# Opening of a diffusion trunk: the first four k-slices of four row tiles' query, key and value products between the adaLN products, and 256 rows of x loaded later

## The chip, the cores and the metric

The kernel runs on one core of one Trainium2 chip. The metric is device microseconds of one execution. Before the change three runs took 2756.55, 2757.89 and 2761.49 us; the median is 2757.89 us.

## The reference

A trunk of two layers over 1024 latent rows (x, 1024 channels) and 256 context rows. Layer 0 mixes by neighbourhood attention, layer 1 by sliding-window attention; each ends with a gated ConvFFN. Only the beginning of layer 0 matters here:

```python
mod = silu_c @ w_mod[i] + b_mod[i]
mod_c = silu_cc @ w_mod[i] + b_mod[i]
sh1, sc1, gt1, sh2, sc2, gt2 = jnp.split(mod[:, None, :], 6, axis=-1)
h = modulate(rmsnorm(x, g_attn[i]), sh1, sc1)
hc = modulate(rmsnorm(ctx, g_attn[i]), sh1c, sc1c)
q, k, v = attn_inputs(h, w_in, gq, gk, n_kv)
q_c, k_c, v_c = attn_inputs(hc, w_in, gq, gk, n_kv, with_q=not last)
```

So every row of h needs the shift and scale (sh1, sc1), which come out of a product with the 1024 x 2048 left part of w_mod, and every product of queries, keys and values sums over all 1024 channels of h.

## The kernel before

**Tiling.** Rows stand in ten tiles of 128: tiles 0 to 7 are x, 8 and 9 the context. Channels stand in eight slices of 128 (kt 0 to 7, `KT`). Float32 products are made of three passes: each operand is split into a rounded part and a rest (`whi`, `wlo` of the weights, `h0hi`, `h0lo` of h for x, `h0chi`, `h0clo` for the context), and hi*hi, lo*hi and hi*lo are summed in one PSUM bank. `plan_qkv_mm` plans a row tile's product for one pair of heads: eight steps kt of three matmuls of 384 columns, into a bank `mm`. Ten tiles make a head pair (`hp`), eight pairs make the layer; `ORDER` is 8, 9, 0, ..., 7.

**Opening** (the block that opens the pool `x0`, L883 on). The list `so` holds its steps. `plan_x` loads row tiles, sums their squares (ScalarE, `junk<-xt`), scales the rows (`times`), transposes them to channels by rows and evicts them to `x`; it does so for the context (8, 9) and for tiles 0 to 3 together. `plan_mods(half)` multiplies SiLU(c) with eight 512 KB pieces `wm` of w_mod; half 0 gives shift and scale for kt 0 to 3, half 1 for kt 4 to 7; the sum goes through ScalarE (`modsb`), a transpose (`modt`) and VectorE (`modc`). `plan_apply` turns `x` into `h0hi` and `h0lo` for one kt: an affine step, a cast and a subtraction. Four weight pieces of the first head pair (`slab`, two kt each) are loaded and split there too, the first two ahead of the second half of w_mod, the others behind it.

**After the opening** the list `sc` runs: the products of all row tiles, the attention of each head pair, and, ahead of them, `plan_norm0`, which brings tiles 4 to 7 (loaded behind everything else) to `h0hi` and `n1lo`: four sums of squares, four row scalings, eight groups of four transposes into banks `pt`, eight evictions with shift and scale (`t`, the last two into `S`), eight casts, eight subtractions. Its subtractions all wait for the last transpose, since `n1lo` takes the place of the rows themselves.

**What sets the order.** `Sched.op` records a step with an engine (or several to choose from), an assumed duration, what it reads and writes, and a key; `Sched.run` takes the steps as their inputs come free, smallest key first, and writes out one fixed order for each engine. At run time each engine goes through its order and waits where an input is late. DMAs stand in one queue, SP's, in the order of their keys.

Of the kernel before, what the change touches and what calls it, by code (L numbers as in the profile page):

```python
# [17 lines left out]
P = 128  # L18
D = 1024
# [204 lines left out]
def trunk_kernel(ctx, tc, xtok, xseq, cc, crow, wmod, wmodt, bmod, gnorm, na_wqkv, na_gqk, na_bias, na_wo,  # L224
# [29 lines left out]
    dma.dma_start(cpad[:, :, 0:2], cc)  # L254
# [16 lines left out]
    act.activation(cpad[:, :, 0:2], cpad[:, :, 0:2], AF.Silu)  # L271
# [181 lines left out]
    def plan_qkv_mm(sc, key, psa, h, tt, slabs, s, J, c0=0, hkey=None):  # L453

        hh, hl = h[tt // 4]
        sl = slice((tt % 4) * P, (tt % 4) * P + P)
        for kt in range(KT):
            def mm(e, kt=kt):
                if kt == 0:
                    J["acc"] = psa("mm", F32)  # L460
                wh, wl = [a[:, kt % 2, c0:384] for a in slabs.get(4 * s + kt // 2)]
                for i, (a, w) in enumerate(((hh, wh), (hl, wh), (hh, wl))):
                    pe.matmul(J["acc"][:, c0:384], a[:, kt, sl], w, start=(kt == 0 and i == 0),
                              stop=(kt == KT - 1 and i == 2))
# [3 lines left out]
                  acq=[("mm", J["id"] + ("acc",), 1)] if kt == 0 else (), rel=[("w", i)] if kt % 2 else ())  # L468
# [207 lines left out]
    def plan_norm0(sc, psa, wk, junk, xt, hl, key):  # L676

        B = {}
        K = lambda *a: ("n1",) + a

        def sq(e, q):
            if q == 0:
                for s in "vyt":
                    B[s] = tiny.tile([P, 4], F32, tag="n1" + s, name="n1" + s, bufs=1)
            act.activation(junk, xt[q], AF.Square, scale=1.0 / 32.0, accum_out=B["v"][:, q:q + 1])
        for q in range(4):
            sc.op("act", t_act(D) + 0.19, lambda e, q=q: sq(e, q), reads=[("x1", q)] + ([K("ms", q - 1)] if q else []),
                  writes=[K("ms", q)], key=key, rel=["sums1"] if q == 3 else [])
# [11 lines left out]
        def times(e, q):  # L700
            if e == "act":
                act.activation(xt[q], xt[q], AF.Copy, scale=B["y"][:, q:q + 1])
            else:
                dve.tensor_scalar(out=xt[q], in0=xt[q], scalar1=B["y"][:, q:q + 1], scalar2=None, op0=ALU.mult)
        for q in range(4):
            sc.op(("dve", "act"), (0.8, t_act(D)), lambda e, q=q: times(e, q), reads=[K("y")], writes=[("x1", q)], key=key)
        for k in range(KT):
            hi, ring = hl[0][:, k, :], "pt5" if k < 6 else "S"
            shift, scale = modc[:, 0, 0, 0, k:k + 1], modc[:, 0, 0, 1, k:k + 1]

            def tr(e, k=k):
                B["p", k] = psa("pt", F32)
                for q in range(4):
                    pe.transpose(B["p", k][:, q * P:(q + 1) * P], xt[q][:, k * P:(k + 1) * P], idf)
            sc.op("pe", 0.44, tr, reads=[("x1", q) for q in range(4)], writes=[K("tr", k)], key=key, acq=[("pt", K("tr", k), 1)])

            def t(e, k=k, ring=ring, shift=shift, scale=scale):
                if ring == "S":
                    B["t", k] = SP["pool"].tile([P, SP["n"]], F32, tag="S", name="S", bufs=SBUFS)[:, :512]
                else:  # L720
                    B["t", k] = wk.tile([P, 512], F32, tag="pt5", name="t", bufs=PTB["pt5"])
                if e == "act":
                    act.activation(B["t", k], B["p", k], AF.Identity, bias=shift, scale=scale)
                else:
                    dve.tensor_scalar(out=B["t", k], in0=B["p", k], scalar1=scale, scalar2=shift, op0=ALU.mult, op1=ALU.add)
            sc.op(("act", "dve"), (t_actp(512), t_dve(512)), t, reads=[K("tr", k)], writes=[K("t", k)], key=key, rel=[K("tr", k)],
                  acq=[(ring, K("t", k), 1)])

            def hif(e, k=k, hi=hi):
                if e == "act":  # L730
                    act.activation(hi, B["t", k], AF.Copy)
                else:
                    dve.tensor_copy(hi, B["t", k])
            sc.op(("act", "dve"), (t_act(512), 0.45), hif, reads=[K("t", k)], writes=[K("hi", k)], key=key)
        for k in range(KT):
            def lof(e, k=k):
                if k % 2 == 0:
                    hl[1].tiles[k // 2] = lo_part("n1lo")
                dve.tensor_tensor(out=hl[1][:, k, :], in0=B["t", k], in1=hl[0][:, k, :].bitcast(F32), op=ALU.subtract)
            sc.op("dve", t_dve(512), lof, reads=[K("hi", k)] + [K("tr", j) for j in range(KT)] + ([("h0", 1, k - 1)] if k % 2 else []),  # L740
                  writes=[("h0", 1, k)], key=key, rel=[K("t", k)])
# [141 lines left out]
    with tc.tile_pool(name="x0", bufs=1, reuse_waits="tile") as xp, \  # L883
            tc.tile_pool(name="ps0", bufs=1, space=PS, reuse_waits="tile") as ps:
        CUT = {2: (8, 9), 0: (0, 1, 2, 3)}
        xc = {0: hpool.tile([P, KT, 512], F32, tag="hhi", name="x0", bufs=2),
              2: xp.tile([P, KT, TC], F32, name="x2")}
        xt = {i: xp.tile([P, D], F32, tag="xt", name=f"xt{i}", bufs=6) for c in (2, 0) for i in CUT[c]}
        tiny.tile([P, 32], F32, name="pad", bufs=1)
# [14 lines left out]
        for n, i in enumerate((8, 9)):  # L904
            load(1.34, -100 + n, [("xt", i)], lambda i=i: dma.dma_start(xt[i], xtok[i]))
        load(0.3, -98, [("bg",)], lambda: (dma.dma_start(bmod_t, bmod), dma.dma_start(gn, gnorm)))
        for i in range(4):
            load(1.34, -95 + i, [("xt", i)], lambda i=i: dma.dma_start(xt[i], xtok[i]))
# [16 lines left out]
        def tr_bank():  # L925
            return ps.tile([P, 512], F32, tag="tr", name="tr", bufs=4)

        def plan_x(c):
            tl, n, b = CUT[c], CH[c][1], 10 * (c == 0)
# [3 lines left out]
            def sq(e, q, i):  # L933
# [3 lines left out]
                act.activation(junk, xt[i], AF.Square, scale=1.0 / 32.0, accum_out=MS[c, "v"][:, q:q + 1])  # L937
# [1719 lines left out]
```

## Time and profile before

| | |
|---|---|
| profiled execution, device time | 2756.76 us |
| its span | 2754.6 us |
| median of three runs | 2757.89 us |
| TensorE (PE) busy | 2695.8 us, 98% |
| VectorE (DVE) busy | 2247.3 us, 82% |
| ScalarE (ACT) busy | 1685.4 us, 61% |
| GpSimd (POOL) busy | 339.9 us, 12% |
| mean of the 16 DMA engines | 141 GB/s |

The busy shares are means over stages that differ. In the first of the page's 40 slices of 69 us PE is busy for seven tenths and the DMA engines move 263 GB/s; in nearly all others PE is at nine tenths or more. A timeline gives the start, the length and the name of an instruction or of a run of equal ones, and in brackets how long the engine was idle before it and what ended that. Instructions on one engine overlap a little: their pace is the distance of two starts, not the length.

### The profile page before, as it was taken

Reading aid. Unit: us, or ns where it says so; the run is one execution under the profiler, and the core shown is the slowest. Engines: PE = TensorE matmul, PEld = TensorE weight load, DVE = VectorE, ACT = ScalarE, POOL = GpSimd, SP = SyncE. Lnnn points to the kernel's source line nnn. Section 1 sums busy time; section 2 is a strip of 40 time slices with the busy share of each in tenths; the row PEclk is TensorE's granted clock in tenths of the full one; section 3 lists DMA queues with packets and bytes.
Section 4 is the critical chain, followed back from the end, with each engine's and each line's share of the span. In section 5 each row is a group of like instructions: output and inputs, shape, how many; then the busy total and the mean of one; then the engine's idle time right before and its main releaser. Section 6 shows DMA issues by size and latency. Waiting matters only on the chain.

```text
span 2754.6 us, 42728 instructions
## 1 busy us (share of the span) xinstructions
PE 2695.8 (98%) x15300; PEld 2277.4 (83%) x15300; DVE 2247.3 (82%) x4938; ACT 1685.4 (61%) x3000; POOL 339.9 (12%) x520
## 2 busy tenths in 40 slices
PE   7999999998999999999999999999999999999999
PEld 5999999987799988887888877777778788888887
DVE  5988888887788688787886889898877988888757
ACT  6777777776456555555564556666754666656433
POOL 1211111112000000000001007455410000000000
PEclk9999999999999999999999999999999999999999
DMA  7343343325656543334375662143253233334655
GB/s 263 98 127 120 114 136 117 111 91 175 211 173 185 183 142 106 128 118 134 123 252 190 191 197 68 43 129 102 77 154 110 88 115 101 112 108 147 230 174 187
DMA packets 149180, 387.89 MB, mean 141 GB/s; under 512 B 21476, under 2 KB 34276, under 8 KB 148584
## 3 DMA queue, kind: packets, MB, share of 16 engines
q1 hardware_dynamic: 148968, 385.17, 43.2%
q8 instruction: 120, 1.97, 0.3%
q14 instruction: 92, 0.75, 0.1%
HBM read 318.12 MB, written 66.99 MB: 140 GB/s over the span
## 4 chain that ended last, share of the span: by engine, by line
PE 66%; DVE 5%; DMA 2%; issue 1%; POOL 1%; ACT 1%; SPq 0%; DVEq 0%; ACTq 0%; POOLq 0%
PE ua L51 17%; PE uc L51 13%; PE dn L51 13%; PE mm L51 5%; PE oacc L51 4%; PE pt L51 4%; PE ud L51 4%; PE dnc L51 2%; PE s L51 2%; DVE S L51 1%; DVE wlo L51 1%; DVE xn L51 1%; PE ug L51 0%; POOL qa L51 0%; DMA c_dram<-cx 0%
## 5 line engine op out<-in xcount | busy, mean ns | idle before, releaser
L51 ACT ACTIVATE whi<-wraw 128x512 fp32r<-128x512 f32 (+1 forms) x264 | 212.3, 804 | 149.6 <-PE uc L51 57.5
L51 DVE TENSOR_TENSOR wlo<-wraw,whi 128x512 fp32r<-128x512 f32 (+1 forms) x264 | 240.8, 912 | 46.6 <-ACT whi L51 46.1
L51 ACT ACTIVATE S<-S,m 128x640 f32<-128x640 f32 (+3 forms) x288 | 220.8, 768 | 63.4 <-DVE m L51 44.9
L51 PE MATMUL dn<-ghi,whi 128*128 128x512 f32 x616 | 240.2, 390 | 0.1
L51 PE MATMUL dn<-glo,whi 128*128 128x512 f32 x616 | 239.9, 389 | 0.2 <-DVE glo L51 0.2
L51 PE MATMUL dn<-ghi,wlo 128*128 128x512 f32 x616 | 239.8, 389 | 0.0
L51 ACT ACTIVATE whi<-s 128x1024 fp32r<-128x1024 f32 (+1 forms) x118 | 111.0, 941 | 181.5 <-PE uc L51 99.7
L51 POOL TENSOR_TENSOR qy<-qv,mhalf 128x4 f32<-128x4 f32 (+1 forms) x114 | 135.3, 1188 | 597.7 <-DVE qv L51 572.6
L51 PE MATMUL pt<-idr,S 128*128 128x128 f32 x1288 | 194.3, 277 | 12.1 <-DVE S L51 6.1
L51 PEld LDWEIGHTS pt<-idr,S 128*128 128x128 f32 x1288 | 151.2, 141 | 46.9 <-issue 11.7
L51 ACT ACTIVATE ghi<-graw 128x512 fp32r<-128x512 f32 x154 | 95.8, 629 | 150.9 <-PE dn L51 91.2
L51 PE MATMUL mm<-whi,h0hi 128*128 128x384 f32 x512 | 180.1, 352 | 0.0
L51 ACT ACTIVATE pt<-pt 128x512 f32<-128x512 f32 (+2 forms) x259 | 133.4, 535 | 64.6 <-PE pt L51 62.7
L51 PE MATMUL mm<-wlo,h0hi 128*128 128x384 f32 x512 | 172.1, 336 | 0.0
L51 DVE TENSOR_TENSOR glo<-graw,ghi 128x512 fp32r<-128x512 f32 x154 | 105.0, 690 | 80.9 <-ACT ghi L51 50.9
L51 DVE TENSOR_TENSOR wlo<-s,whi 128x1024 fp32r<-128x1024 f32 (+1 forms) x118 | 127.0, 1078 | 21.2 <-ACT whi L51 20.8
L51 PEld LDWEIGHTS dn<-ghi,whi 128*128 128x128 f32 x616 | 115.6, 188 | 24.9 <-ACT ghi L51 0.5
L51 PEld LDWEIGHTS dn<-glo,whi 128*128 128x128 f32 x616 | 115.7, 188 | 24.4 <-DVE glo L51 0.5
L51 PE MATMUL ua<-t12hi,whi 128*128 128x512 f32 x344 | 134.8, 392 | 0.8 <-ACT c L51 0.8
L51 PEld LDWEIGHTS dn<-ghi,wlo 128*128 128x128 f32 x616 | 115.6, 188 | 24.1
L51 PE MATMUL ua<-t12lo,whi 128*128 128x512 f32 x344 | 134.0, 390 | 0.0
L51 PE MATMUL ua<-t12hi,wlo 128*128 128x512 f32 x344 | 133.9, 389 | 0.0
(372 smaller groups left out, 8291.3 us busy)
## 6 DMA issues: line engine op xcount, KB each, us to landing
wraw<-in_w_up_dram SPq DMA_DIRECT2D x133, 512.0 KB, 3.8
wmt<-in_wmodt_dram SPq DMA_DIRECT2D x96, 512.0 KB, 4.1
wraw<-in_w_down_dram SPq DMA_DIRECT2D x44, 512.0 KB, 3.8
graw<-g_dram SPq DMA_DIRECT2D x44, 512.0 KB, 4.4
wraw<-in_w_down_dram SPq DMA_DIRECT2D x88, 256.0 KB, 3.0
graw<-g_dram SPq DMA_DIRECT2D x66, 256.0 KB, 2.7
wm<-in_wmod_dram SPq DMA_DIRECT2D x32, 512.0 KB, 8.7
slab<-in_na_wqkv_dram SPq DMA_DIRECT2D x32, 384.0 KB, 3.1
```

What stands on the lines that cost most here:

```text
L51: r = f(*a, **k)
```

## The change

The context and tiles 0 and 1 are prepared in the opening as before; tiles 2 and 3 no longer are. Their rows are loaded behind w_mod, and a second use of `plan_norm0` brings them to h after the opening (`c == "b"`, groups of two row tiles, 256 columns per kt). The step list of the opening gets half of `plan_qkv_mm` (kt 0 to 3) for tiles 8, 9, 0 and 1 (`EARLY`); they hold two banks `mm` and two banks `s` until the second list adds kt 4 to 7. For that the PSUM pool of the attention is opened before the opening. Slabs 2 and 3 get keys inside the second half of w_mod, `cr` and `cpad` (the two rows of c) are loaded behind the context rows. The squares of tiles 4 to 7 get key 2.5 in place of -100. The subtractions may go to POOL as well.

```diff
-        CUT = {2: (8, 9), 0: (0, 1, 2, 3)}
+    EARLY, EA = {8: 'mm', 9: 'mm', 0: 's', 1: 's'}, {}
+        CUT = {2: (8, 9), 0: (0, 1)}
...
-        dma.dma_start(cr, crow)
-        act.activation(cr, cr, AF.Silu)
+        load(0.2, -99, [("cr",), ("cp",)], lambda: (dma.dma_start(cr, crow), dma.dma_start(cpad[:, :, 0:2], cc)))
+        so.op("act", 1.05, lambda e: act.activation(cr, cr, AF.Silu), reads=[("cr",)], writes=[("cr",)], key=-10)
...
-        for i in range(4):
-            load(1.34, -95 + i, [("xt", i)], lambda i=i: dma.dma_start(xt[i], xtok[i]))
+        for i in range(2):
+            load(1.34, -78 + i, [("xt", i)], lambda i=i: dma.dma_start(xt[i], xtok[i]))
...
-            load(1.0, (-80, -79, -60, -59)[i], [("raw", i)], lambda i=i: slabs.load(i), acq=[("raw", ("raw", i), 2)])
+            load(1.0, (-80, -79, -72.5, -68.5)[i], [("raw", i)], lambda i=i: slabs.load(i), acq=[("raw", ("raw", i), 2)])
-        for i in range(4, 8):
+        for i in range(2, 8):
             load(1.34, -55 + i, [("xt", i)], lambda i=i: dma.dma_start(xt[i], xtok[i]))
...
+        plan_sums0(so, junk, xt, (2, 3), "b", 39)
+        for tt, tag in EARLY.items():
+            J = EA[tt] = dict(id=("q0", 0, tt))
+            plan_qkv_mm(so, 100 + 10 * (tt < 8) + tt % 4, psa, h, tt, slabs, 0, J, 0, ("h0", tt // 4), tag, 0, KT // 2)
         so.run()
...
+        early = hp == 0 and tt in EARLY
+        J = EA[tt] if early else dict(id=I)
+        if early:
+            sc.hold(EARLY[tt], I + ("acc",), 1)
+        plan_qkv_mm(sc, key, psa, h, tt, slabs, hp, J, 0, hkey, k0=KT // 2 if early else 0)
...
-            sc.op("dve", t_dve(512), lof, reads=[K("hi", k)] + [K("tr", j) for j in range(KT)] + ([("h0", 1, k - 1)] if k % 2 else []),
-                  writes=[("h0", 1, k)], key=key, rel=[K("t", k)])
+            sc.op(("dve", "pool"), (t_dve(512), 1.4 * t_pool(512)), lof, reads=[K("hi", u)] + ([K("tr", j) for j in range(KT)] if c == 1 else []) +
+                  ([("h0", 1, u - 1)] if c == 1 and u % 2 else []), writes=[("h0", c, u * m + a) for a in range(m)], key=key,
+                  rel=[K("t", u)])
...
-    plan_norm0(sc, psa, wk, sums0, [xt[i] for i in range(4, 8)], h[1], -100)
+    plan_norm0(sc, psa, wk, xt, h, (2, 3), "b", -150)
+    plan_sums0(sc, sums0, xt, (4, 5, 6, 7), 1, 2.5, ["sums1"])
+    plan_norm0(sc, psa, wk, xt, h, (4, 5, 6, 7), 1, 2.5, [("n0", "b", "tr", u) for u in range(KT // 2)])
```

The planner moves many instructions. Buffer names follow the source: `pt`, `s`, `mm` and `pv` are PSUM banks, `cpad` is SiLU(c), `modsb` the sum of a half of w_mod's products.

PE around the last piece of w_mod, before:

```order
L51 MATMUL mod_327<-wm_368,cpad 32x256 x4
L51 MATMUL mod_327<-wm_377,cpad 32x256 x4
L51 MATMUL modt<-idr,modsb_401 128x128 x2
L51 MATMUL mm<-whi,h0chi 128x384
L51 MATMUL mm<-whi,h0clo 128x384
L51 MATMUL mm<-wlo,h0chi 128x384
```

and with the change (wm_388 is the last piece, h0hi_119 belongs to tiles 0 to 3):

```order
L51 MATMUL s<-whi,h0hi_119 128x384
L51 MATMUL s<-whi,h0lo_121 128x384
L51 MATMUL s<-wlo,h0hi_119 128x384
L51 MATMUL pt<-wm_388,cpad 32x256 x4
L51 MATMUL s<-whi,h0hi_119 128x384
L51 MATMUL s<-whi,h0lo_121 128x384
L51 MATMUL s<-wlo,h0hi_119 128x384
L51 MATMUL s<-whi,h0hi_119 128x384
L51 MATMUL s<-whi,h0lo_120 128x384
L51 MATMUL s<-wlo,h0hi_119 128x384
L51 MATMUL pv<-idr,modsb_427 128x128 x2
```

Before, the first product of h stands behind the last product of w_mod; now all 24 of the context and nine of tiles 0 and 1 stand ahead of it, and six more between it and its transpose.

ACT behind the sum of the second half (`modsb`), before:

```order
L51 ACTIVATE whi<-slab 128x768 x2
L51 ACTIVATE x_111<-x_111,modc 128x256 x2
L51 ACTIVATE h0chi<-x_111 128x256 x2
L51 ACTIVATE x_111<-x_111,modc 128x256
L51 ACTIVATE x_110<-x_110,modc 128x512
```

and with the change (x_108 holds tiles 2 and 3 here, x_109 the context):

```order
L51 ACTIVATE modsb_427<-pt 128x256
L51 ACTIVATE junk,nbv<-x_108 128x1024 x2
L51 ACTIVATE h0chi<-x_109 128x256
L51 ACTIVATE x_109<-x_109,modc 128x256
L51 ACTIVATE h0chi<-x_109 128x256 x2
L51 ACTIVATE x_108<-x_108,modc 128x256 x2
L51 ACTIVATE h0hi_119<-x_108 128x256
L51 ACTIVATE x_108<-x_108,nby 128x1024
```

The two splits of slabs have gone ahead of `modsb`; two sums of squares, of tiles 2 and 3, stand there now, and a row scaling further on.

PE where tile 3 is done and tiles 4 to 7 come up, before (x_119 to x_122 are tiles 4 to 7):

```order
L51 MATMUL mm<-wlo,h0hi_123 128x384
L51 MATMUL pt<-idr,x_119 128x128
L51 MATMUL pt<-idr,x_120 128x128
L51 MATMUL pt<-idr,x_121 128x128
L51 MATMUL pt<-idr,x_122 128x128
```

and with the change (x_115 to x_118 are tiles 4 to 7, the last product is tile 3's last):

```order
L51 MATMUL mm<-wlo,h0hi_119 128x384
L51 MATMUL s<-kkc,q 128x256
L51 MATMUL s<-klc,q 128x256
L51 MATMUL s<-kkc,q 128x256
L51 MATMUL s<-klc,q 128x256
L51 MATMUL pt<-idr,x_115 128x128
L51 MATMUL pt<-idr,x_116 128x128
L51 MATMUL pt<-idr,x_117 128x128
L51 MATMUL pt<-idr,x_118 128x128
```

Before, the transposes stand between the products of tiles 2 and 3; now all 32 stand behind them, with the first scores of the context, and the products of tile 4 follow. On ACT a table load stands between the evictions of these transposes, and three of the eight subtractions stand on POOL. Behind the first head pair (from about the 660th row of PE's order and the 350th of DVE's) both orders are the same to the end.

## Rows read from the trace of the kernel before

**Rows 1.** Busy time by stretch: us; busy (instructions) of PE, PEld, DVE, ACT, POOL; clock, DMA, GB/s
```profile
15.00:20.00 5.00, 3.28 (x38) 1.09 (x30) 2.10 (x7) 2.57 (x3) 1.01 (x1) 1.00 1.05 395
...
25.00:30.00 5.00, 2.25 (x30) 1.39 (x26) 4.30 (x14) 5.00 (x11) 0.00 (x0) 1.00 1.05 388
...
35.00:39.70 4.70, 3.53 (x26) 0.89 (x27) 0.00 (x0) 0.72 (x2) 0.00 (x0) 0.50 1.04 404
39.70:45.00 5.30, 5.30 (x26) 5.30 (x25) 4.54 (x15) 5.30 (x12) 0.00 (x0) 0.78 0.74 294
...
400.00:500.00 100.00, 100.00 (x697) 91.91 (x696) 87.40 (x309) 74.78 (x176) 14.50 (x14) 1.00 0.41 131
```

**Rows 2.** Timeline of SP's DMA issues, opening: start us, us, queue, line, what
```profile
0.74 0.37 SPq L51 DMA_DIRECT2D cr<-in_crow_dram  x1
...
1.86 1.11 SPq L51 DMA_DIRECT2D xt<-in_xtok_dram  x2
```

**Rows 3.** Timeline of PE around the last pieces of w_mod
```profile
36.48 1.08 PE L51 MATMUL mod<-wm,cpad 128*32 128x256 f32 x8 [0.27 <-DMA wm<-in_wmod_dram]
37.83 1.08 PE L51 MATMUL mod<-wm,cpad 128*32 128x256 f32 x8 [0.27 <-DMA wm<-in_wmod_dram]
...
39.75 0.67 PE L51 MATMUL mm<-whi,h0chi 128*128 128x384 f32 x1
...
41.82 0.42 PE L51 MATMUL mm<-whi,h0chi 128*128 128x384 f32 x1
```

**Rows 4.** Timeline of PE from the transposes of tiles 4 to 7 to tile 4
```profile
59.09 1.04 PE L51 MATMUL pt<-idr,x 128*128 128x128 f32 x8
...
70.53 0.33 PE L51 MATMUL mm<-wlo,h0hi 128*128 128x384 f32 x1
70.70 0.33 PE L51 MATMUL mm<-whi,h0hi 128*128 128x384 f32 x1
...
73.82 0.28 PE L51 MATMUL s<-kkc,q 128*128 128x256 f32 x1
...
74.29 0.34 PE L51 MATMUL mm<-whi,h0hi 128*128 128x384 f32 x1
```

**Rows 5.** Timeline of ACT, 27 to 77 us
```profile
27.36 1.08 ACT L51 ACTIVATE x<-x,modc 128x256 f32<-128x256 f32 x2
28.35 0.71 ACT L51 ACTIVATE h0chi<-x 128x256 fp32r<-128x256 f32 x2
...
47.42 1.04 ACT L51 ACTIVATE sums<-x 128x1024 f32<-128x1024 f32 x1
...
48.46 0.47 ACT L51 ACTIVATE qraw<-mm 128x384 f32<-128x384 f32 x1
...
56.51 1.14 ACT L51 ACTIVATE x<-x,n1y 128x1024 f32<-128x1024 f32 x1
...
64.72 0.78 ACT L51 ACTIVATE S<-pt,modc 128x512 f32<-128x512 f32 x1
65.39 0.48 ACT L51 ACTIVATE qraw<-mm 128x384 f32<-128x384 f32 x1
...
75.52 1.28 ACT L51 ACT_TABLE_LOAD   x1
76.82 0.51 ACT L51 ACTIVATE S<-S,m 128x256 f32<-128x256 f32 x1
```

**Rows 6.** Timeline of DVE: the subtractions of tiles 4 to 7, and two equal casts
```profile
66.92 3.09 DVE L51 TENSOR_TENSOR n1lo<-t,h0hi 128x512 fp32r<-128x512 f32 x5
...
95.15 1.43 DVE L51 CAST kll<-kll 64x256 fp32r<-64x256 f32 x1
...
97.25 0.29 DVE L51 CAST kll<-kll 64x256 fp32r<-64x256 f32 x1
```

**Rows 7.** Timeline of POOL, 94 to 99 us
```profile
94.62 1.81 POOL L51 TENSOR_TENSOR wlo<-slab,whi 128x768 fp32r<-128x768 f32 x1 [1.37 <-ACT whi L51]
```

**Rows 8.** Timeline of PE, 96 to 98 us
```profile
97.08 0.33 PE L51 MATMUL pt<-idr,S 128*128 128x128 f32 x1 [1.48 <-DVE kll L51]
```

More of the change, by code (lines that the diff above doesn't have):

```diff
@@ L451, in plan, with plan_qkv_mm @@
                   writes=[("wl", i)], key=key - 2, rel=[("raw", i)])
[L453 to L455 removed]
+    def plan_qkv_mm(sc, key, psa, h, tt, slabs, s, J, c0=0, hkey=None, bank="mm", k0=0, k1=KT):
         sl = slice((tt % 4) * P, (tt % 4) * P + P)
[L457 removed]
+        for kt in range(k0, k1):
             def mm(e, kt=kt):
                 if kt == 0:
[L460 removed]
+                    J["acc"] = psa(bank, F32)
+                hh, hl = h[tt // 4]
                 wh, wl = [a[:, kt % 2, c0:384] for a in slabs.get(4 * s + kt // 2)]
@@ L707, in plan_norm0 @@
[L707 to L719, printed above, removed]
-                else:
-                    B["t", k] = wk.tile([P, 512], F32, tag="pt5", name="t", bufs=PTB["pt5"])
+                dve.tensor_scalar(out=xt[i], in0=xt[i], scalar1=B["y"][:, q:q + 1], scalar2=None, op0=ALU.mult)
@@ L729, in hif @@
-            def hif(e, k=k, hi=hi):
-                if e == "act":
-                    act.activation(hi, B["t", k], AF.Copy)
-                else:
[L733 to L739, printed above, removed]
-            sc.op("dve", t_dve(512), lof, reads=[K("hi", k)] + [K("tr", j) for j in range(KT)] + ([("h0", 1, k - 1)] if k % 2 else []),
-                  writes=[("h0", 1, k)], key=key, rel=[K("t", k)])
+                    dve.tensor_copy(hi, tv(u))
@@ new lines, in plan_norm0, with lof @@
+            sc.op(("act", "dve"), (t_act(512), 0.45), hif, reads=[K("t", u, a) for a in range(m)] + list(after)
+                  + ([K("hi", 0)] if u else []), writes=[K("hi", u)], key=key)
+        for u in range(KT // m):
+            def lof(e, u=u):
+                hl = h[tl[0] // 4]
+                if c == 1:
+                    if u % 2 == 0:
+                        hl[1].tiles[u // 2] = lo_part("n1lo")
+                    lo = hl[1].tiles[u // 2][:, u % 2:u % 2 + 1, :]
+                else:
+                    lo = hl[1].tiles[u][:, :, c0:c0 + n]
+                ENG[e].tensor_tensor(out=lo, in0=tv(u), in1=cols(hl[0], u).bitcast(F32), op=ALU.subtract)
+            sc.op(("dve", "pool"), (t_dve(512), 1.4 * t_pool(512)), lof, reads=[K("hi", u)] + ([K("tr", j) for j in range(KT)] if c == 1 else []) +
+                  ([("h0", 1, u - 1)] if c == 1 and u % 2 else []), writes=[("h0", c, u * m + a) for a in range(m)], key=key,
+                  rel=[K("t", u)])
@@ L892, in trunk_kernel @@
         h = [hi_lo("h0", 0), None, hi_lo("h0", 2)]
-        junk = xp.tile([P, D], F32, name="junk")
+        junk = [xp.tile([P, D], F32, name="junk") for _ in range(2)]
         cr = xp.tile([P, D], F32, name="cr")[0:2]
-        dma.dma_start(cr, crow)
-        act.activation(cr, cr, AF.Silu)
-        so = Sched(dict(tr=4, raw=3, wm=12))
-        so.op("dma", 2.5, lambda e: None, key=-1000)
+        so = Sched(dict(PSB, raw=3, wm=12))
+        so.op("dma", 1.5, lambda e: None, key=-1000)
         def load(dur, key, w, f, **kw):
```

162 lines of the change are left out of this document (103 added, 59 removed).

## The prediction

> **What bounds the kernel now.** I read the page first (PE 98% busy, the others well below), then the busy time by stretch, then the timelines of SP, PE, ACT, DVE and POOL up to 100 us, then the order of both programs. From the second head pair on PE is the bound: it is busy for 100.00 of the 100 us from 400 to 500 [rows 1]. The opening is bound by loads: the pieces of w_mod land 1.35 us apart, PE takes each one as it lands, and from 35 to 39.7 us all that PE does is wait for the next [rows 1, 3]. The first product of h starts at 39.75, and for two more us the products run slowly. So PE time before 39.75 is free, and what the change puts there is PE work out of a stage in which PE is the bound. The question is whether PE can use what it saves. For that I look at the next place where it needs something new: tile 4, whose first product starts at 70.70 [rows 4].
>
> **The loads.** The first row tile is issued at 0.74 instead of 1.86 us, since the two small loads of c go behind it [rows 2]: 1.1 us. Ahead of the last piece of w_mod stood six row tiles, sixteen pieces of 512 KB and two slabs of 384 KB; now there are four, sixteen and four, 256 KB less, at 1.35 us for 512 KB [rows 3] another 0.7 us. The small loads have to pass all the same, 0.2 us. The last piece should start its product at 37.83 - 1.6 = 36.2 us, within 0.9 to either side. SP's order has one new wait: slab 3 needs slab 0's buffer, so it waits for a subtraction on DVE, with the last piece of w_mod queued behind it. By my count that subtraction ends about 2 us before SP gets there, so I cost it at nothing; if that cover went, each us of it would delay everything below by one.
>
> **PE's own side.** A product pass takes 0.17 us at full clock [rows 4]. 48 passes of the first four kt of four tiles move ahead of 39.75; nine of them stand behind the last transpose of the modulation, so 39 are done, 6.7 us. Against that, 16 transposes of tiles 2 and 3 come behind, at about 0.13 us each by the eight in 1.04 us [rows 4]: 2.1 us. There are two new waits, because h for kt 4 to 7 of the context is now needed at once, where before eight us of products covered it: I put them at 1.6 us. With the earlier loads PE alone would reach the end of tile 3 four to five us ahead.
>
> **ACT's side, which I take to decide.** Tile 4 needs the whole of the second `plan_norm0`, and ACT carries most of it. In the new order ACT, once the modulation is summed, first takes the squares of tiles 2 and 3, which land 1.35 us behind the last piece, so from about 37.6 us. From there to its last eviction for tiles 4 to 7 its order holds six sums of squares at 1.04 us (6.2), three affine steps of 256 columns at 0.5 (1.5), seven casts of 256 at 0.31 (2.2), three row scalings at 1.1 (3.3), six evictions of 512 columns at 0.67 (4.0), two casts of 512 at 0.5 (1.0), six evictions of 256, which no row shows: between the cast's 0.31 and the affine step's 0.5, I take 0.45, nearest to the latter (2.7). Add eighteen small steps on queries and keys of the other tiles, at the 384-column eviction's 0.47 less the 0.1 by which neighbours overlap (6.7), the table load at 1.28 and one exponential at 0.5 (1.8) [rows 5]. Sum 29.4 us. With 1.5 us of waits, for the load of tile 3's rows and for transposes, ACT is through at 68.5 us. The first subtraction and tile 4's first product follow at about 69.1.
>
> Before, that product started at 70.70, with the same products and transposes done but not the eight score passes of the context, which stand ahead of it now: four of them take 0.47 us [rows 4], so 0.94. The gain at that point is 1.6 + 0.94 = 2.5 us, not the four to five that PE alone would have.
>
> **Two smaller terms.** The eight subtractions ran on DVE, five in 3.09 us [rows 6]; three of them go to POOL, which needed 1.81 us for 768 columns [rows 7], so 1.2 us each for 512. While POOL worked on that piece, DVE's cast took 1.43 us where an equal one took 0.29 [rows 6, 7]; DVE has two such casts between POOL's subtractions now. Tile 4's products want a new kt each 0.52 us, so PE loses between 0.4 and 1.7 us here; I take 1.0, midway. On the other hand the POOL subtraction at 94.62 is the one that held DVE up and led to PE's stall of 1.48 us at 97.08 [rows 7, 8]; in the new order POOL has no slab there. DVE has it instead, at 0.95 us, so what is won is between nothing and 1.5 us; I take 0.8.
>
> **The sum.** 2.5 - 1.0 + 0.8 = 2.3 us. Bounds with the 0.9 us of the loads: 2.5 - 1.7 - 0.9 = -0.1 and 2.5 - 0.4 + 1.5 + 0.9 = 4.5 us. Behind the first head pair every engine's order is what it was and PE is the bound, so the shift passes to the end. Against the profiled execution that is 2756.76 - 2.3 = 2754.5 us. The median of the runs stands 1.1 us above that execution, so I forecast **2755.6 us**, with the case's own bounds at 2753.4 and 2758.0.
>
> ACT gets a second table load at its start, because the squares now run ahead of the SiLU; the load-bound stretch behind covers its 1.28 us. The load in the middle of the evictions is the one that costs. In the row the exponential starts 0.02 us after the table load ends [rows 5], so I cost it at 1.28. The Trainium skill says more (ScalarE: Activation LUTs, "What ACT_TABLE_LOAD costs"): a switch of sets is the load of about 1283 ns and a drain of about 1380 ns. By that the gain would be some 0.9 us instead of 2.3. The trace agrees on the load and shows no drain of that size behind it.
>
> **The rivals.**
> (a) *PE decides, not ACT.* If ACT's small steps cost less than I count, or DVE takes evictions over in its idle time, PE reaches tile 4 by its own work: from 38.3 us, 105 passes (18.1), 56 transposes at 0.13 (7.3), the scores (0.9), waits of 1.6 make 66.2, a gain of 70.7 + 0.9 - 66.2 = 5.4, with the stall of rows 8 up to 6.9 us: 2752.5 to 2751.0. For it: PE has the work in hand. Against it: ACT is in order and its sum leaves no room for four us.
> (b) *The early products hold up the weights.* PE takes its order strictly, and nine passes stand between the last two pieces of w_mod. From 25 to 30 us PE was busy for 2.25 of 5 us; after that its granted clock fell, to 0.50 from 35 to 39.7 us, which is 1.2 GHz [rows 1]. At that clock a piece takes 1.08 us [rows 3], nine passes at 0.32 us 2.9, more than the 1.35 between two pieces: the last one would start 1.6 us late, which takes the loads' gain away. 2.3 - 1.6 = 0.7: 2757.2 us. For it: PE is idle for some us in the new order too, while it waits for the first context h. Against it: from 24 us on it has more to do than before.
> (c) *Slower.* Between tiles 3 and 4 PE now runs dry: the transposes come as fast as ACT empties two banks, where before they stood among products. If PE's clock falls there, tile 4 begins at 1.2 GHz. Before, the low clock lasted from the dense work's start at 37.83 to 41.82 [rows 3], 4.0 us, at half the pace: a loss of 2.0 us. With the loads no earlier (tile 4 at 70.7), it is 0.94 - 2.0 - 1.0 = -2.1 us: 2760.0 us. It decides if tile 4 begins after 69.6 us at the low clock. For it: eight us at less than half load. Against it: from 15 to 20 us PE was busy for 3.28 of 5 us and the clock stayed at 1.00 [rows 1]. The Trainium skill (TensorE: Matmul & The Clock Gate, Part 1) has the throttled state as the default, released by activity, which speaks for this rival; by that rule alone the price is the same 2.0 us.
>
> **How the numbers follow.** Forecast 0.60, (a) 0.12, (b) 0.14, (c) 0.14. A measurement of this kernel tells about 0.2%, 5.5 us, from no change: below 2752.4 counts as faster, above 2763.4 as slower. The forecast, (b) and most of (c) lie between. Of (a) most is faster by more, 0.10, and a tail of the forecast adds 0.02: faster 0.12. Slower by more needs (c) with a late slab 3 on top: 0.03. Same 0.85. The three runs before spread over 5 us, so medians of three move by 1 to 2; the range is the forecast's bounds widened by 1.7 us on either side and stretched to the near end of (a): 2751.0 to 2759.7.
>
> **What would show it.** Right: the last piece's product at 36 us, squares of `nbv` on ACT at 37 to 40, the clock at full before 38, tile 3's last product at about 60, then PE mostly idle with transposes among ACT's evictions, the first `n1lo` product near 69, and no stall at 97. Wrong: `n1lo` products at 66 (a), the last piece at 37.8 behind slow passes (b), 384-column passes 0.32 us apart behind 69 us (c), or orders that agree while PE's waits past 100 us differ by more than 1 us.

## The result, and the profile after the change

Over 22 runs the changed kernel took 2762.65 us in the median, the kernel before 2758.03 over as many beside it: a ratio of 1.0017, with an interval of 1.0011 to 1.0024. It is slower by some 4.6 us, less than the 0.2% named in the prediction; 2762.65 lies above the prediction's upper bound of 2759.7. The profiled execution of the changed kernel took 2761.46 us, its span is 2759.7 us; PE 2706.4 us busy, DVE 2248.8, ACT 1686.0, POOL 346.4.

Busy time by stretch, changed kernel, columns as in [rows 1]:

```profile
20.00:25.00 5.00, 1.87 (x11) 0.99 (x11) 4.25 (x13) 4.61 (x9) 0.60 (x1) 0.52 1.04 394
25.00:30.00 5.00, 5.00 (x40) 2.88 (x32) 1.76 (x6) 1.99 (x2) 0.10 (x1) 0.80 1.04 389
...
35.00:39.70 4.70, 4.70 (x36) 3.34 (x35) 0.96 (x1) 1.83 (x3) 0.00 (x0) 1.00 1.03 410
...
65.00:70.00 5.00, 3.28 (x17) 2.31 (x17) 3.19 (x9) 4.85 (x10) 0.00 (x0) 0.79 0.00 0
70.00:75.00 5.00, 3.55 (x18) 2.57 (x17) 4.71 (x6) 4.48 (x11) 3.42 (x3) 0.86 0.00 0
```

Before, PE was busy without a gap from 40 to 80 us. Now it is saturated from 25 to 40 us instead, and runs dry from 65 to 75, while ACT is at 4.85 of 5 us. The clock falls twice: from 20 to 30 us, and around 70.

Timeline of PE, changed kernel:

```profile
23.13 0.69 PE L51 MATMUL mm<-whi,h0chi 128*128 128x384 f32 x1 [3.59 <-ACT h0chi L51]
...
35.58 0.64 PE L51 MATMUL pt<-wm,cpad 128*32 128x256 f32 x8
36.15 0.45 PE L51 MATMUL s<-whi,h0hi 128*128 128x384 f32 x1
...
37.94 0.64 PE L51 MATMUL pt<-wm,cpad 128*32 128x256 f32 x8
...
61.52 0.34 PE L51 MATMUL mm<-wlo,h0hi 128*128 128x384 f32 x1
...
67.97 3.14 PE L51 MATMUL pt<-idr,x 128*128 128x128 f32 x12 [1.12 <-ACT t L51]
...
71.65 0.42 PE L51 MATMUL mm<-whi,h0hi 128*128 128x384 f32 x1
72.42 0.44 PE L51 MATMUL mm<-whi,n1lo 128*128 128x384 f32 x1 [0.35 <-DVE n1lo L51]
...
74.79 0.44 PE L51 MATMUL mm<-whi,n1lo 128*128 128x384 f32 x1 [1.04 <-DVE n1lo L51]
...
76.48 0.44 PE L51 MATMUL mm<-whi,n1lo 128*128 128x384 f32 x1 [0.37 <-DVE n1lo L51]
```

Tile 3 is done at 61.52, nine us earlier than before [rows 4]. But the last piece of w_mod still starts its product at 37.94 (37.83 before [rows 3]), nine early passes behind the piece ahead of it, and tile 4 starts at 71.65, 0.95 us later than before, with the eight scores of the context done. Its 24 passes then wait three times for `n1lo`.

ACT, whose chain leads to tile 4:

```profile
38.92 1.05 ACT L51 ACTIVATE junk<-x 128x1024 f32<-128x1024 f32 x1
...
65.36 1.28 ACT L51 ACT_TABLE_LOAD   x1
66.65 0.51 ACT L51 ACTIVATE S<-S,m 128x256 f32<-128x256 f32 x1
...
71.15 0.78 ACT L51 ACTIVATE S<-pt,modc 128x512 f32<-128x512 f32 x1
```

The subtractions of tiles 4 to 7, on DVE and on POOL:

```profile
71.02 1.35 DVE L51 TENSOR_TENSOR n1lo<-t,h0hi 128x512 fp32r<-128x512 f32 x1
...
72.96 4.66 DVE L51 TENSOR_TENSOR n1lo<-t,h0hi 128x512 fp32r<-128x512 f32 x4
```
```profile
70.55 1.27 POOL L51 TENSOR_TENSOR n1lo<-t,h0hi 128x512 fp32r<-128x512 f32 x1 [5.76 <-PE pt L51]
72.85 3.02 POOL L51 TENSOR_TENSOR n1lo<-S,h0hi 128x512 fp32r<-128x512 f32 x2 [1.03 <-DVE h0hi L51]
```

On DVE one took 0.62 us before [rows 6]. Beside POOL's, the one at 71.02 takes 1.27 us to the next start and the first two of the four at 72.96 take 1.69 and 1.70; the last two, behind the end of POOL's work at 75.87, take 0.60 again.

**A measure for what follows.** Orders differ from kernel to kernel, so equal times don't mean equal work. *PE's lag* at a time t is t less the work that PE has begun by then, each instruction counted with the usual distance of two starts for its shape (0.173 us for 384 columns, 0.109 us for a transpose); extra passes of an experiment are not counted as work. The table's columns give the lag less that of the kernel before at the same time: negative is ahead. It wavers by some tenths with the mix of instructions; behind 250 us orders agree for most kernels and it is the difference in time.

| kernel | lag at 40 | 60 | 80 | 530 us | median, us | ratio to before (interval) |
|---|---|---|---|---|---|---|
| changed | -4.7 | -4.3 | +3.3 | +4.1 | 2762.65 | 1.0017 (1.0011 to 1.0024) |
| x13 changed, again | -4.7 | -4.3 | +3.6 | +4.1 | 2760.87 | 1.0011 (1.0002 to 1.0019) |
| x1 subtractions on DVE | -3.8 | -3.4 | +3.1 | +3.8 | 2759.56 | 1.0005 (0.9996 to 1.0014) |
| x2 no early products | -1.4 | +1.5 | +3.1 | +3.5 | 2760.04 | 1.0006 (0.9998 to 1.0015) |
| x4 dry stretch filled | -3.7 | -3.3 | +4.0 | +4.2 | 2758.13 | 1.0004 (0.9995 to 1.0013) |
| x5 squares twice | -3.5 | -2.0 | +5.7 | +5.5 | 2763.95 | 1.0024 (1.0015 to 1.0034) |
| x7 squares on DVE | -4.2 | -3.6 | +7.1 | +4.7 | 2763.92 | 1.0024 (1.0015 to 1.0033) |
| x8 norm first | -3.3 | -2.5 | +2.4 | +4.2 | 2761.27 | 1.0011 (1.0002 to 1.0020) |
| x9 early exponential | -3.5 | -2.9 | +2.7 | +4.2 | 2759.95 | 1.0008 (0.9999 to 1.0017) |
| x10 opening filled | -5.3 | -4.7 | +2.7 | +4.1 | 2759.89 | 1.0009 (1.0000 to 1.0018) |
| x11 three mends | -5.3 | -4.9 | +0.2 | +1.1 | 2759.10 | 1.0003 (0.9994 to 1.0012) |
| x14 mends, context only | -2.0 | -0.7 | -0.1 | +2.0 | 2757.61 | 1.0000 (0.9991 to 1.0009) |
| x18 mends, norm first | -3.9 | -3.4 | +1.0 | +2.7 | 2756.77 | 0.9999 (0.9990 to 1.0008) |

So the place of most of the loss is plain: the changed kernel is 4.3 us ahead at 60 us and 3.3 behind at 80. Behind that the lag still grows in most kernels, by up to 2.1 us (x14) to 530 us.

### The profile page after: what moved, and what is told of

The parts are those of the page before. It is cut to its first block, busy times and chain, and to the rows that moved or that the text cites. A ratio compares the mean times of both kernels' runs of the same rounds, so it can differ in the third digit from the quotient of the medians.

```text
span 2759.7 us, 42763 instructions
## 1 busy us (share of the span) xinstructions
PE 2706.4 (98%) x15300; PEld 2282.1 (83%) x15300; DVE 2248.8 (81%) x4948; ACT 1686.0 (61%) x3008; POOL 346.4 (13%) x524
## 4 chain that ended last, share of the span: by engine, by line
PE 78%; DVE 7%; DMA 2%; issue 2%; ACT 1%; POOL 1%; SPq 0%; DVEq 0%; ACTq 0%; POOLq 0%
PE ua L51 17%; PE dn L51 13%; PE uc L51 13%; PE mm L51 11%; PE pt L51 6%; PE oacc L51 4%; PE ud L51 4%; PE s L51 4%; PE dnc L51 2%; PE pv L51 2%; DVE S L51 1%; DVE wlo L51 1%; DVE xn L51 1%; PE ug L51 0%; POOL qa L51 0%
## 5 line engine op out<-in xcount | busy, mean ns | idle before, releaser
L51 PE MATMUL mm<-whi,h0hi 128*128 128x384 f32 x496 | 174.1, 351 | 0.0
```

The lines of the kernel that those rows point to most:

```text
L51: r = f(*a, **k)
```

## The experiments

My theory (T) was that the loss is made between tiles 3 and 5 because the second norm ends late; R1 that the early products cost the time; R2 that it is the new order behind tile 4.

**x1, subtractions back on DVE**

```diff
-                ENG[e].tensor_tensor(out=lo, in0=tv(u), ...
+                ENG["dve" if c == 1 else e].tensor_tensor(out=lo, in0=tv(u), ...
```

> The three subtractions for tiles 4 to 7 that POOL took go back to DVE, in the same place of the order; PE's and ACT's orders are those of the changed kernel. Theory T (the loss is made between the end of tile 3 and the end of tile 4: the second norm ends late, its subtractions are stretched, and PE runs dry): tile 4's first product stays near 71.6 us, its 24 passes take 5.1 us instead of 6.8 (the three waits of 0.35, 1.04 and 0.37 us shrink), and the time falls by 1.0 to 1.8 us against the changed kernel, to about 2761. Rival R1 (the early products themselves cost the time): no change, 2762 to 2763. Rival R2 (the loss lies in the order behind tile 4): tile 4 ends earlier, but the gain is gone by 150 us; 2762 to 2763.

DVE, x1:

```profile
74.39 1.89 DVE L51 TENSOR_TENSOR n1lo<-t,h0hi 128x512 fp32r<-128x512 f32 x3
```

The pace is 0.63 again, tile 4's passes take 5.5 us from first to last instead of 6.8, and one wait of 0.55 is left of three. POOL's help was a loss of 1.3 us there, as T had it. At 530 us the gain is hidden by an opening that was 0.9 us slower in this profile; the median is 3.1 lower than the changed kernel's, and 1.3 lower than in its repeat x13, with overlapping intervals.

**x2, no early products; x3, early products alone.** x2: `EARLY` empty. x3: `CUT`, loads and keys of the kernel before, `EARLY` kept.

> The rest of the change without the 48 early passes: all 96 passes of the first four tiles stand behind the modulation. T: the last w_mod piece's product starts at 36.3 us instead of 37.9 and ACT's second part 1.3 us earlier, but PE has 8.2 us more to do behind it, so tile 3 ends near 68 us, PE does not run dry, and tile 4 starts at 70 to 71.5, its clock full; the time is 2759 to 2761.5, between both kernels. R1: with the early products gone the time is that of the kernel before or less, 2756 to 2758. R2: 2762 to 2763, as the changed kernel.

> The early products alone: tiles 2 and 3 keep their place in the opening (loaded ahead of the weights, normed together with tiles 0 and 1), and the second norm stands where it was in the kernel before. T: ACT has no norm of tiles 2 and 3 in its way, so the second norm is through earlier than in the changed kernel; tile 4 starts between 66 and 69.5 us and the time is 2753 to 2757. R1: the passes between the last pieces of w_mod hold up the weights; tile 4 starts at 71 or later and the time is 2760 or more. R2: 2760 to 2763, since the order behind tile 4 is planned anew here too.

x2's last piece of w_mod starts at 36.74 (T: 36.3), but PE then idles for 1.63 us before the first product of h, and the clock falls:

```profile
40.00:45.00 5.00, 5.00 (x15) 4.75 (x16) 4.59 (x17) 3.07 (x8) 0.69 (x1) 0.50 0.77 272
```

It loses most at 40 to 50 us, at that clock, and some at 66 to 73 us, where PE waits for the norm; it ends at about the lag of the changed kernel. R1 falls: without the early products the rest of the change is no faster, and with them it is no slower. The 5.8 us by which the changed kernel is further at 60 us (-4.3 against +1.5) are simply not on the path at 80 us. x3 took 2776.47 us (1.0064, 1.0051 to 1.0076), but it says little of its question: its lag was +2.3 at 80 and +6.5 at 530, in an order of its own, and of the rest at least a part came from moved addresses (below).

**x4, the dry stretch filled with extra passes**

```diff
+            if c == 1 and u > 0:
+                sc.op("pe", FILL * t_pe(384), fill, reads=[K("tr", u)], writes=[K("fill", u)], key=key,
+                      acq=[("pv", K("fill", u), 1)], rel=[K("fill", u)])
```

> Five extra 384-column passes into a spare bank behind each of the last seven transposes of tiles 4 to 7, results unused: PE has work while it waits for ACT's evictions. The passes come on top of the computation. T with the clock (PE runs dry, the granted clock falls to half at 67.9 us, and the last transposes take 3.1 us where 1.6 would do): the granted clock stays at 1.00 from 65 to 75 us, tile 4 starts 0.5 to 1.3 us earlier than in the changed kernel, and the time falls by that, to 2761 to 2762. If the clock costs nothing, since ACT decides: tile 4 starts where it did (71.6) or up to 0.6 later by the extra passes, 2762.5 to 2763.5. R1 and R2: no gain either.

The clock stayed at 1.00 from 60 to 80 us, yet tile 4 began at 73.90 and the lag is no better. The median of 2758.13 is lower than the profile explains. So the profile shows no gain from the clock there. x15 and x16 below, with three such passes each, can't tell: in x14 and x11 the clock stays at 1.00 there without them.

**x5, ACT made longer; x7, ACT made shorter at DVE's cost; x8, the norm's rank.** x5: `square(...)` called twice for tiles 4 and 5. x7: `sc.op("dve" if q % 2 and c == 1 else "act", ...)` for the squares. x8: keys of `plan_sums0` and `plan_norm0` of tiles 4 to 7 from 2.5 to -100.

> ACT takes the squares of tiles 4 and 5 twice: two more instructions of 1.06 us with their accumulator reads, 2.35 us in all, and every engine's order else that of the changed kernel. If ACT's chain from the modulation to the last eviction of tiles 4 to 7 sets the start of tile 4 (T), that start moves from 71.6 to about 73.8 us and the time rises by 1.9 to 2.4, to 2764.5 to 2765. If something else sets it (loads, PE's own order, the order behind tile 4: R1, R2), the start stays and the time rises by 0.5 at most.

> The squares of tiles 5 and 7 go to DVE, which is busy for 3 to 4 of 5 us there: 2.35 us less on ACT, and some other steps change engines behind it. T: tile 4 starts 1.2 to 2.3 us earlier than in the changed kernel and the time falls by as much, 2760.3 to 2761.5. Rival: DVE becomes the bound (it has the casts, row scalings and subtractions of the same norm) and the start stays at 71 to 72; no gain.

> The sums and the norm of tiles 4 to 7 get the rank that they had in the kernel before, ahead of the small steps on queries and keys of the first four tiles. T: the evictions and transposes for tiles 4 to 7 run among the products of tiles 0 to 3, which cover them; PE runs dry for under 1 us between 60 and 72 us, tile 4 starts at 66 to 68.5, and the time is 2757.5 to 2760.5, since the delayed small steps cost PE some waits behind 75 us. R2 (the order behind tile 4 costs the time): 2761 or more, although tile 4 starts earlier.

PE, x5:

```profile
74.41 0.42 PE L51 MATMUL mm<-whi,h0hi 128*128 128x384 f32 x1
```

Tile 4 starts at 74.41, and the lag at 80 is 2.4 higher than in the changed kernel for 2.35 us of work on ACT; but 1.2 of that stands at 40 us already, since the opening was slower in this profile. Against x9, whose lag at 40 is equal, it is 3.0 for 2.35 plus the table load's 1.28. From its first square to its last eviction ACT waits for 1.75 us in x5, for 2.5 in the changed kernel: part of the added work went into waits, the rest moved tile 4. ACT's chain is the path there, if not quite one for one. x7 went the other way, as its rival said: the squares take 1.22 us on DVE, the row scalings behind them start at 64.59 instead of 57.20, and tile 4 starts at 76.35. In x8 tile 4 starts at 68.31, but then PE waits for what has been put off:

```profile
71.92 0.44 PE L51 MATMUL mm<-whi,n1lo 128*128 128x384 f32 x1 [0.90 <-DVE n1lo L51]
...
83.58 0.45 PE L51 MATMUL mm<-whi,h0hi 128*128 128x384 f32 x1 [1.40 <-ACT qraw L51]
...
100.52 0.98 PE L51 MATMUL pt<-idr,S 128*128 128x128 f32 x7 [1.42 <-DVE S L51]
```

From 45 to 105 us ACT and DVE are busy for 46.9 and 51.9 of 60 us in the changed kernel: what x8 brings forward there delays other steps.

**x6 and x9, the table load moved; x12, addresses moved.** x6 puts one exponential into the opening, with a tile of 32 bytes for its result; x9 does the same with the tile `pad`, which is there and unread; x12 is the kernel before with `pad` 32 bytes wider.

```diff
+        so.op("act", 1.5, lambda e: act.activation(warm[:, :1], mhalf[:, :1], AF.Exp), reads=[("cr",), ("cp",)], writes=[("warm",)], key=-9)
```

> One exponential of a single column in the load-bound opening, its result unused, so that the table load of 1.28 us between ACT's evictions for tiles 4 to 7 (at 65.36 us) is done there already; every other order is that of the changed kernel. T: the evictions behind it come 1.28 us earlier, tile 4 starts at 70.3 to 70.7 us and the time falls by 0.8 to 1.3, to about 2761.5. If ACT is not what decides: no change, 2762.6.

> The early exponential of the run before, but into a tile that is there already and that nothing reads, so that no address of the memory moves by its 32 bytes. In the run with a tile of its own the start of tile 4 did move (70.98 us with an opening 1.3 us later), but the passes of the down projections (1440 to 1610 us and from 2560 us on) took about 3% longer, 7 us in all. If that came from the moved addresses (theory A): those passes are as in the changed kernel, and the time is 2761 to 2762.5. If it came from the table load's new place or the exponential (theory B): 2769 again. Of the table load itself: tile 4 starts 1.3 us earlier for an equal opening; the end gains under 0.5, since DVE then waits for a load of the next modulation's weights (wmt) near 106 us, which stands where it stood.

> The kernel before with the unread tile of the opening 32 bytes wider; the instructions are the same on every engine. Theory A (the addresses set the pace of the down projections): 3% on those passes, 5 to 8 us more than the kernel before, 2763 to 2766. Theory B: the same as the kernel before, 2758.

x6 took 2769.00 us (1.0038, 1.0026 to 1.0051), x9 2759.95, x12 2765.24 (1.0029, 1.0020 to 1.0038). Busy time from 1450 to 1600 us, in layer 0's second part: the kernel before, x6, x9 and x12, in this order.

```profile
1450.00:1600.00 150.00, 150.00 (x672) 124.42 (x671) 119.48 (x193) 74.21 (x125) 4.83 (x4) 1.00 0.58 185
```
```profile
1450.00:1600.00 150.00, 150.00 (x656) 121.87 (x655) 114.95 (x185) 71.99 (x122) 8.44 (x7) 1.00 0.59 187
```
```profile
1450.00:1600.00 150.00, 150.00 (x671) 124.45 (x670) 118.40 (x188) 73.63 (x124) 8.51 (x7) 1.00 0.60 192
```
```profile
1450.00:1600.00 150.00, 150.00 (x657) 121.68 (x656) 117.12 (x190) 73.05 (x124) 2.54 (x3) 1.00 0.58 181
```

PE is busy all the time at the full clock, but does 2% fewer passes in x6 and x12. The instructions of x12 are those of the kernel before; only addresses moved. So theory A holds, and x6 and x3 (655 there) can't be read by their end. The changed kernel has 671: it did not lose this way. Of the table load, x9 shows the gain at 80 us: 0.6 lower than the changed kernel with an opening 1.2 slower, so some 1.8 us. Not all of it need be the load's 1.28, since the granted clock also stayed at 1.00 from 65 to 75 us in x9. The end shows none of it.

**x10, PE kept busy in the opening; x11, three mends together**

```diff
+            for n in range(7 if tt == 8 else 0):
+                def fill(e, n=n, J=J):
+                    if n == 0:
+                        J["acc"] = psa("mm", F32)
+                    for _ in range(4):
+                        pe.transpose(J["acc"][:, :P], xt[8][:, :P], idf)
+                so.op("pe", 0.44, fill, reads=[("mod", 0, "tp")], writes=[J["id"] + ("acc",)], key=-20,
+                      acq=[("mm", J["id"] + ("acc",), 1)] if n == 0 else ())
```

> 28 extra transposes, results unused, fill PE's 3.6 us of idleness ahead of the first h0c product at 23.1 us; every other order is that of the changed kernel. Theory C (PE's idleness there lets the granted clock fall to half until 27 to 30 us, and since PE is saturated from 23 to 38 us, the last w_mod piece waits behind passes that would have been done): the clock stays at 1.00 from 20 to 30 us, the last w_mod piece starts its product at 36.2 to 36.5 us instead of 37.9 to 39, the second norm and tile 4 come 1.3 to 2.5 us earlier, and the time is 2760 to 2761.5. Rival: the last piece waits for its load or for the nine passes all the same; no change, 2762.6 or up to 0.4 more.

> Three edits together: the three subtractions back on DVE, the early exponential in the unread tile, and the fill of PE in the opening. T: each shortens the way to the end of tile 4 (1.3, 1.3 and 1.3 to 2.5 us), so PE's lag behind the kernel before at 80 us, 3.3 us in the changed kernel, falls to between -1 and 1, and if nothing else holds the time it is 2757 to 2759. Rival D (a second bound behind it: DVE's wait for the wmt loads at 106 us, which SP issues at 101.6 instead of 96.5 us): tile 4 ends 3 us or more earlier, but the lag at 120 us is back at 3 to 3.5, and the time is 2760 to 2761.5.

Busy time by stretch, x10, against the first two rows of the changed kernel above:

```profile
20.00:25.00 5.00, 4.68 (x37) 3.87 (x41) 4.35 (x15) 5.00 (x10) 0.00 (x0) 1.00 1.03 390
25.00:30.00 5.00, 4.75 (x42) 2.94 (x35) 2.52 (x8) 2.67 (x5) 0.70 (x1) 1.00 1.04 390
```

PE, x10, and busy time of x9, which has the changed kernel's order of PE and no fill:

```profile
37.51 0.64 PE L51 MATMUL pt<-wm,cpad 128*32 128x256 f32 x8
```
```profile
25.00:30.00 5.00, 5.00 (x31) 2.19 (x30) 1.87 (x6) 2.03 (x3) 0.53 (x1) 0.54 1.05 389
```

The clock stays up, as theory C has it, but the gain is small: the last piece starts at 37.51, behind its nine passes, and not at 36.2 to 36.5. But for the fill, PE's order is that of the changed kernel, and from 30 to 100 us the same instruction comes 0.4 us earlier, at 530 us no earlier; the rival was nearer. The price of the low clock differs between profiles. In eleven profiles of kernels with all 48 early products (x3, whose loads differ, left out) it fell in the opening, and the last piece started at 37.86 to 39.70, for the most part later where the mean clock from 25 to 30 us was lower: 37.94 at 0.80 in the changed kernel, 39.28 at 0.54 in x9. In x10 and x11 it did not fall, and the piece started at 37.51 and 37.45. x16 and x18 have the fill too, but PE waited 1.15 and 0.91 us for a load near 25 us and the clock fell to a mean of 0.66 from 25 to 30.

x11 adds the two other mends. It is 3.1 us better than the changed kernel at 80 us, with a lag of +0.2, as T has it, and 3.0 at 530. So the three mends take back nearly all of what is lost by 80 us. The median of 2759.10 (T: 2757 to 2759) can't be told from the kernel before. Rival D falls: the wmt operation on DVE came at 102.71 instead of 106.25, along with everything else.

**x13 to x18.** x13 is the changed kernel again. x14 is x11 with `EARLY = {8: 'mm', 9: 'mm'}`; x15 and x16 are x14 and x11 with x4's fill at three passes; x17 and x18 are x14 and x11 with x8's keys.

> The changed kernel itself, once more. If its first profile had a lucky opening: the last w_mod piece's product starts at 38.9 to 39.4 us instead of 37.94, PE's lag behind the kernel before at 80 us is 4.0 to 4.6 us instead of 3.3, tile 4 starts at 72.5 to 72.9. If not: 37.9, 3.3 and 71.6 again. The median is 2762 to 2763 either way.

> The three edits of the run before, and early products for the two context tiles alone (24 passes; those of tiles 0 and 1 go back behind the modulation), so no pass of tiles 0 and 1 stands between the last pieces of w_mod. Rival b as a cost of its own: the last piece starts at 36.2 instead of 37.5 us, ACT's chain 1.3 us earlier, tile 4 at 68 to 68.5 instead of 69.2 and the lag at 80 us up to 1 us lower; median 2757.5 to 2759. If the 24 passes are needed as work before 38 us: PE reaches the end of tile 3 some 2.8 us later (64 us), still ahead of ACT, and tile 4 starts at 69 or later; 2758.5 to 2760.

> As the run before, and three extra passes behind each of the last seven transposes of tiles 4 to 7, results unused (21 passes, 3.6 us of PE time, on top of the computation). If the clock falls in the dry stretch and costs (theory C there): it stays at 1.00 from 60 to 75 us and the time falls by up to 1 us against x14 in spite of the extra work. If ACT's chain alone decides: the same as x14 or up to 1.5 us more.

> The three edits with all 48 early products, and the 21 extra passes. Against x11 (2759.1): the same two cases, 2758 to 2759 if the clock costs there, 2759 to 2760.5 if it does not. Below the kernel before (2757.6) only if the lead of 1.9 us that x11 has at 530 us is kept to the end.

> x14 (three mends, early products for the context tiles alone) with the sums and the norm of tiles 4 to 7 ranked ahead of the small steps on queries and keys, as in the kernel before. In its order 33 passes of tile 3 and the ones before it still stand behind the last transpose for tiles 4 to 7. T: these cover the rest of the norm, PE does not run dry at all between 45 and 80 us, and its lead over the kernel before at 80 us is the 4 to 5 us that x14 has at 40 us (x14 keeps 3.1); the median is 2755 to 2757. Rival: the delayed small steps make PE wait behind 80 us as in x8 (1.4 and 1.4 us), the lead at 150 us is 2 or less, and the median is 2757.5 or more.

> x11 (three mends, all 48 early products) with the same rank. Its lead is 8 us at 40 to 60 us. T: the cover is thinner here, since 24 passes more are gone before 38 us: PE runs dry for some 2 to 4 us before tile 4, the lead at 80 us is 3 to 5 us, and the median is 2756 to 2759. Rival: as in x17.

The expectations of x16 to x18 speak of leads in which the 28 extra transposes, some 3 us, are counted as work; by the table's measure x11 is 5.3 us ahead at 40 us and 1.1 behind at 530, and x14 is 2.0 ahead at 40 and 0.1 at 80.

x13: the last piece starts at 37.86, so my doubt of the first profile was wrong, though x1, x4, x5, x7 and x8, with the same opening, have it at 38.58 to 39.67. The lags of both profiles agree to 0.4 us up to 530 us. Behind that they part by 3.3 us in the end. In the first profile the clock falls near 1641 and near 2003 us, in x13 it does not, and there the first loses 1.3 and 0.8 us on the second. The first profile, then x13:

```profile
1640.00:1650.00 10.00, 8.96 (x45) 8.71 (x46) 9.50 (x21) 5.35 (x11) 0.00 (x0) 0.83 0.48 145
2000.00:2010.00 10.00, 7.74 (x39) 4.88 (x37) 9.39 (x27) 6.75 (x14) 5.12 (x14) 0.83 0.24 80
```
```profile
1640.00:1650.00 10.00, 9.58 (x60) 9.58 (x61) 10.00 (x19) 6.27 (x12) 0.00 (x0) 1.00 0.38 120
2000.00:2010.00 10.00, 9.20 (x62) 6.21 (x62) 9.42 (x33) 7.67 (x16) 4.49 (x13) 1.00 0.16 55
```

With such differences a median of 11 runs need not follow a lag of 2 us at 530. In x14 the last piece waits for its load, and starts 0.5 us earlier than in x11, so the nine passes cost about 0.5 there:

```profile
36.92 0.64 PE L51 MATMUL pt<-wm,cpad 128*32 128x256 f32 x8 [0.71 <-DMA wm<-in_wmod_dram]
```

PE starts the last pass of tile 3 at 68.80 and tile 4 at 70.80, 1.6 us later than x11, but tile 4's passes take 4.4 us instead of 5.9: half of the early products serve about as well as all of them. From 80 to 530 us the lag goes from -0.1 to +2.0; the median of 2757.61 us is even with the kernel before. x15 took 2761.10 (1.0015, 1.0006 to 1.0024) and x16 2758.99 (1.0004, 0.9996 to 1.0013): the extra passes buy nothing, and there was no low clock for them to lift. x17 took 2758.21 (1.0004, 0.9995 to 1.0013); PE waits for the norm for 0.9 us at 58 and 59 us, the scores wait for `klc` at 71 to 74 us, and PE is some 3 us behind at 80. x18 is 1.0 us behind at 80 and 2.7 at 530; its 2756.77 is the lowest median, and can't be told from the kernel before. No version that I ran beats it measurably, and by the table none is ahead of it at 530 us. R2 is thus right in part: the new orders lose something behind tile 4 as well. No run takes that part by itself.

## Why the prediction was wrong, step by step

- *The loads, "36.2 us"*: the load itself came about when forecast (in x2, x14, x15 and x17 the product waits for it and starts at 36.35 to 36.92), but in the changed kernel the product starts at 37.94. That is rival (b)'s mechanism at the full clock. The nine passes cost about 0.6 us of the 1.0 behind x14's 36.92 (x10, at the full clock, has 37.51), the clock the other 0.4: PE was idle for 3.59 us ahead of 23.13, its granted clock was 0.52 and 0.80 from 20 to 30 us (1.2 GHz for most of it), and PE, then saturated, carried that backlog along. I had the low clock from 35 us on, where it had been before [rows 1], and not at the new dry place. The Trainium skill (TensorE: Matmul & The Clock Gate, Part 1) has the throttled clock as the default that activity releases; x10 agrees, with 1.00 throughout once transposes fill the gap.
- *PE's own side, "four to five us ahead"*: right; 4.3 us at 60.
- *"ACT's side, which I take to decide"*: right in kind (x5), wrong in size, and this term, with the next, is the step that failed. It was to give a gain of 2.5 us at tile 4 and gave none. From the first square to the last eviction I had 29.4 us of work and 1.5 of waits from 37.6; measured are 30.5 and 2.5 from 38.92. The end is at 71.93 instead of 68.5: 1.3 for the start, 1.1 for work (0.4 of it the six squares, which with their accumulator reads take 1.10 each and not 1.04, 0.3 the eighteen small steps and 0.3 the evictions of 512 columns), 1.0 for waits. Its order has the squares behind `modsb`, so their start hangs on the last piece's product and not on the rows alone. Tile 4 started at 71.65, not 69.1: 2.5 us. It did not wait for the last eviction, which ends at 71.93.
- *Subtractions on POOL, "between 0.4 and 1.7, I take 1.0"*: out of bounds, the other part of the failed step. From its first to its last pass tile 4 took 6.83 us, against 3.99 before without the four scores: 2.8. DVE's and POOL's subtractions gained next to nothing from running side by side: four and two of them took 4.77 us from 72.85 on, where four at 0.62 and two at 1.27 (itself partly beside DVE's) make 5.0 one after the other, and six on DVE alone would make 3.7. The Trainium skill (SBUF — State Buffer, "Who interferes with whom") says that a DVE instruction with two SBUF inputs and a GpSimd instruction that reads SBUF exclude each other. By that rule POOL's share takes nothing off DVE, and the rows agree; x1 gives 1.3 us of it back. I had read the slowed cast [rows 6] as a cost for casts alone.
- *The stall at 97.08, "0.8"*: two waits of 0.42 and 0.33 us stand there now instead of 1.48: 0.7. Right.
- *Table load*: 1.28 us, and the exponential starts 0.01 behind its end: no drain, as forecast.
- *The sum*: -2.3 + 2.5 + 1.8 + 0.1 makes a loss of 2.1 us; the lag at 80 shows 3.3 and at 530 us 4.1. The 2 us between I did not trace to single instructions; their cause stays open.
- *The rivals*: (c) forecast the sign, the dry stretch and the start after 69.6, and its 2760.0 is the nearest number, by luck in good part. Its price, 2.0 us of low clock on tile 4's passes, was not what was paid: in the first profile the clock was back at 71.65, and the lag at 80 is 3.3. In the second (x13) the low clock did fall on tile 4's passes, and the lag at 80 is 3.6:

```profile
75.00:80.00 5.00, 5.00 (x22) 5.00 (x22) 4.83 (x10) 0.42 (x1) 1.06 (x2) 0.71 0.00 0
```

  (b) came true in its place, the last piece 1.7 us behind 36.2, with another cause.

## What to carry to other kernels

Work that is moved ahead of a load pays only if the next serial chain also starts earlier: before moving it, look at what it was covering. A second engine for a step whose instructions read two operands from SBUF on both engines gave nothing here. An extra instruction that fills a gap is not progress: leave it out when you count how far a kernel has got. Look for the new place where PE runs dry, and price the clock there and in the backlog behind it.

## What the runs showed of the hardware

- 32 bytes of address per partition, with not one instruction changed, cost 7.6 us (2765.24 against 2757.62): 2% fewer down-projection passes in the same time at the full clock. In another stage, from 860 to 960 us, x12 does 841 instructions where the kernel before does 836, so some passes get faster. What in the addresses decides was not tried. The kernel before, then x12:

```profile
860.00:960.00 100.00, 100.00 (x836) 100.00 (x835) 68.64 (x105) 53.95 (x82) 0.00 (x0) 1.00 0.61 185
```
```profile
860.00:960.00 100.00, 100.00 (x841) 100.00 (x840) 69.41 (x107) 54.98 (x83) 0.00 (x0) 1.00 0.59 184
```

- Two profiles of one kernel whose lags agree to 0.4 us up to 530 us ended 3.3 us apart, 2.1 of it in two stretches, each behind a wait of PE (0.70 and 1.76 us), where the clock fell in one profile alone.
- The low clock of a dry stretch is paid by what stands behind it in PE's order: with one order of PE (but for x10's fill), the last piece of w_mod started at 37.51 when the clock stayed at 1.00 (x10), at 37.94 with a mean of 0.80 from 25 to 30 us, and at 39.28 with 0.54 (x9).
